# Expert inputs of a mixture-of-experts layer: rows fetched by an indirect DMA in place of one-hot products, and the overflow loop moved behind expert 1

## The chip, the cores and the metric

The program runs on one core of one Trainium2 chip. The metric is device time in microseconds (us) of one execution. The core has TensorE (PE in the profile, with its weight loads as PEld), VectorE (DVE), ScalarE (ACT), GpSimd (POOL) and SyncE (SP), 16 DMA engines that move data between HBM and the on-chip memory SBUF, and the accumulator memory PSUM, which PE writes.

## The reference

A network of four layers on 512 tokens of width 1024, all in float32: two layers of a first block, then two layers of a second block. Only the end of a second-block layer matters here:

```
x = layer_norm(a * x + mix, ln1_g, ln1_b)              # 512 x 1024
f = grouped_moe(x, w_router, router_bias, w_gate, w_up, w_down)
x = layer_norm(a * x + f, ln2_g, ln2_b)
```

`grouped_moe` computes softmax scores over 16 experts in 4 groups, takes the group with the best expert, in it the two best experts for each token, and weights them by their normalised scores. Each expert computes `(silu(x @ w_gate[e]) * (x @ w_up[e])) @ w_down[e]` on its tokens, with `w_gate` and `w_up` 1024 x 512 and `w_down` 512 x 1024. A token's two results, times their weights, are added. Any expert may have any number of tokens; none is dropped.

## The kernel before

Every float32 product is split in three: a value is written as a rounded part h (ACT, `hi`) plus a rest l (DVE, `lo`), and PE computes h*h + h*l + l*h (`mm3`). Weights are split as they arrive.

A second-block layer has two phases. `mix` ends with the product with w_out, the layer norm's statistics, the router and `after_mix` (line 1396), once for token tiles 0 and 1 and once for tiles 2 and 3 (`late`). `after_mix` normalises a tile on ACT, applies the layer norm's scale and shift along the free axis with broadcast tiles, mostly on POOL (`AFFINE`, line 41), and splits the result into `x1` (h and l, 128 tokens x 1024). `route` (line 1507) finds each token's experts and its rank within each expert: `rank` (128 x 4 x 16), ready at the instruction `self.ranked`; then the number of overflow blocks `ovi`, ready at `self.routed`. In layer 0 the second `mem_kv` (keys and values of the memory for layer 1) lies beside it on PE.

`moe` (line 1677) gives each expert a block of 128 rows ("slots") of a DRAM tensor `yd`. Tokens of rank over 128 go to overflow blocks behind the 16 experts' own. First 10 weight chunks of 512 KB are asked for (`first`). Then the overflow loop (line 1688, `For_i` over a count that is read from SBUF into registers of all engines) runs once per overflow block: it gathers tokens, loads the block's expert weights into buffers of its own, and writes its result to `yd`. At the end of the loop, also after no turn at all, all engines wait for each other and for all DMAs in flight.

The gather is `expert_in` (line 1629): for two experts at a time POOL builds a one-hot matrix from `rank` (`expert_slots`), and PE multiplies the tokens' h and l parts by it,

```
nc.tensor.matmul(pt[:, u * n:(u + 1) * n], xs[i][part][:, f], oh[:, i], ...)
```

that is 8 feature tiles x 4 token tiles x 2 parts = 64 products of 256 columns, which leave the two experts' tokens transposed in PSUM. They are split again into `xT`. It stands once ahead of expert 0 and then ahead of each even expert for the next two.

The experts are then walked in order: `expert_up(e)` (48 products of 512 columns in three passes each over 8 feature tiles for gate and up, 4 transposes of the hidden values) and `expert_down(e - 1)` (24 products, two stores of 256 KB into `yd` from ACT's queue). So an expert has 12 weight chunks of 512 KB, 6 products for each. They are loaded by SP's queue, in program order, into 9 buffers: 5 of the tag `mr` and 4 of `wr`; a load waits until its buffer was split by ACT (line 1616) and DVE (line 1617).

At expert 14 POOL adds the two parts of the tokens again into `f` (line 1724), the residual. Expert 15's rows are combined without `yd`; for the others 8 indirect DMAs of POOL (line 1751) fetch each token's two rows of `yd`, and DVE and PE add them, weighted, to `f`.

The framework keeps each engine's instructions near program order, moves up what is ready where an earlier one would wait, and adds the semaphores. `tc.issue_after(x)` keeps an instruction behind x on its engine. What stands behind the loop in the program is not moved ahead of it.

Of the kernel before, what the change touches and what calls it, by code (L numbers as in the profile page):

```python
# [18 lines left out]
P = 128  # L19
T = 512  # L20
D = 1024
# [11 lines left out]
N_OV = 7  # L33
# [4 lines left out]


G, V = ("gpsimd", "gpsimd"), ("vector", "vector")  # L40
AFFINE = ((G, G), (G, G)), ((G, G), (G, V))
T2 = (26, 29, 45, 26)


def slopes(n):
# [3 lines left out]
class K:  # L49
# [1346 lines left out]
    def after_mix(self, l, xs, i0, gb, pl, sc, x1):  # L1396

        nc = self.nc
        tt = nc.vector.tensor_tensor
        st = self.ln_stats(xs[i0:i0 + 2])  # L1400
        u = self.small([2, 16], name="ru2")
        bc = lambda v: v[:, :, None].to_broadcast([P, 2, 16])
        bt = lambda v: v[:, None, :].to_broadcast([P, 2, 16])
        tt(u, bt(self.wsum[:, l, 0]), bc(st[:, 2]), op=OP.mult)
        tt(u, u, bt(self.wsum[:, l, 1]), op=OP.add)
        yield
        c = slice(i0, i0 + 2)
        tt(sc[:, c], pl[:, i0 * 16:(i0 + 2) * 16].rearrange("p (i e) -> p i e", i=2), bc(st[:, 1]), op=OP.mult)
        tt(sc[:, c], sc[:, c], u, op=OP.add)
        yield  # L1410
        late = i0 > 0
        for a in range(2):
            x = xs[i0 + a]
            t = self.x2()
            self.normal(x, st, a)
            for v in range(2):
                eng = AFFINE[late][a][v]
                with self.tc.issue_after(self.ranked.ins) if late else nullcontext():
                    getattr(nc, eng[0]).tensor_tensor(t[v], x[v], gb[0][v], op=OP.mult)  # L1419
                    getattr(nc, eng[1]).tensor_tensor(t[v], t[v], gb[1][v], op=OP.add)  # L1420
            h, lo = [self.wp.tile([P, D], F32R, name="x1", tag="xt", bufs=8) for _ in range(2)]
            x1[i0 + a] = h, lo
            for v in range(2):
                o = slice(v * 512, (v + 1) * 512)
                self.hi(h[:, o], t[v])
                with self.tc.issue_after(self.routed.ins) if late else nullcontext():
                    self.lo(lo[:, o], t[v], h[:, o])

    def moe_constants(self):
        nc, cp = self.nc, self.cp  # L1430
# [12 lines left out]
                                channel_multiplier=-1)  # L1443
# [4 lines left out]
        ap = self.I["router_bias_2"]  # L1448
# [7 lines left out]
        for l in range(2):  # L1456
            for j, name in enumerate(("ln1_g_2", "ln1_b_2")):
                v = self.vec[name, 0][:, l * 8:(l + 1) * 8, None].to_broadcast([P, 8, 16])
# [6 lines left out]
                if j:  # L1465
                    nc.vector.tensor_tensor(s, s, rb, op=OP.add)
        self.yd = self.dp.tile([SLOTS, D], F32, name="yd")

    def clear_slots(self):

# [155 lines left out]
    def f4(self, dt=F32R, name="f4"):  # L1626
        return self.ph.tile([P, D], dt, name=name, tag="f4", bufs=6)

    def expert_in(self, xs, oh, n):

        nc = self.nc
        xT = []
# [12 lines left out]
    def expert_slots(self, rank, e, eng):  # L1645

        oh = self.f4(F32R, "oh").rearrange("p (i a s) -> p i a s", i=4, a=2)
        for a in range(2):
            for i in range(4):
                eng.tensor_scalar(oh[:, i, a], self.iota, rank[:, i, e + a:e + a + 1], None, op0=OP.is_equal)  # L1650
        return oh.rearrange("p i a s -> p i (a s)")

    def expert_up(self, xT, wg, wu):

# [22 lines left out]
    def moe(self, l, xs, rt):  # L1677
# [6 lines left out]

        cur = self.small([P], name="cur", bufs=1)
        nc.vector.tensor_scalar(cur, self.iota, 16.0 * P - 1.0, None, op0=OP.add)
        nov = nc.values_load(ovi[0:1, 7:8], min_val=0, max_val=N_OV)
        with tc.For_i(0, nov, 1) as b:
            ev = nc.values_load(ovi[0:1, bass.ds(b, 1)], engines=[mybir.EngineType.SP], min_val=0, max_val=15)
            row = b * P + 16 * P  # L1690
            we = [w[bass.ds(ev, 1)].rearrange("o k c -> (o k) c") for w in W]
            oh = self.f4(F32R, "oh").rearrange("p (i a s) -> p i a s", i=4, a=2)
            for i in range(4):
                nc.vector.tensor_scalar(oh[:, i, 1], cur, slotf[:, 0, i:i + 1], None, op0=OP.is_equal)
                nc.vector.scalar_tensor_tensor(oh[:, i, 0], cur, slotf[:, 1, i:i + 1], oh[:, i, 1].bitcast(F32),  # L1695
                                               op0=OP.is_equal, op1=OP.add)
            nc.vector.tensor_scalar(cur, cur, float(P), None, op0=OP.add)
            xT = self.expert_in(xs, oh.rearrange("p i a s -> p i (a s)"), 256)
            hT = self.expert_up([[v[:, :P] for v in t] for t in xT], self.wrows(we[0], 8, True), self.wrows(we[1], 8, True))
            self.expert_down(hT, we[2], self.yd[bass.ds(row, P)], True)  # L1700
        oh = self.expert_slots(rank, 0, nc.vector)
        xT = self.expert_in(xs, oh, 256)
        hT = None
        f = []
        for e in range(16):
            if e % 2 == 0 and e < 14:
                oh = self.expert_slots(rank, e + 2, nc.gpsimd)
                nx = self.expert_in(xs, oh, 256)
            if e == 15:
                self.expert_down(hT, W[2][14], self.yd[14 * P:15 * P])  # L1710
            o = e % 2 * P
            h2 = self.expert_up([[v[:, o:o + P] for v in t] for t in xT],
                                *[self.wrows(W[j][e], 8, first=first.pop(0) if first else None) for j in range(2)])
            if e == 2:
                slot, wv, wl = self.weigh(oh1, oh2, sc, slotf)
            if e == 13:
                after = self.last_pe
            if e == 14:
                for i in range(4):
                    with tc.issue_after(after.ins):  # L1720
                        f.append(self.x2())
                        for h in range(2):
                            o = slice(h * 512, (h + 1) * 512)
                            nc.gpsimd.tensor_tensor(f[i][h], xs[i][0][:, o].bitcast(F32), xs[i][1][:, o].bitcast(F32), op=OP.add)
# [3 lines left out]
            if e % 2:  # L1728
                xT = nx

        pt = self.pt()
        for i in range(4):
            nc.tensor.transpose(pt[:, i * P:(i + 1) * P], oh[:, i, P:].bitcast(F32), self.ident)
        ct = self.t2(F32R, "ct")
        nc.scalar.copy(ct, pt)
        pw = self.pt()
        for i in range(4):
            nc.tensor.matmul(pw[:, :1], oh[:, i, P:].bitcast(F32), wl[:, i:i + 1], start=i == 0, stop=i == 3)
        dg = self.t2(F32, "dg")
        for i in range(2):  # L1740
            for j in range(2):
# [14 lines left out]
        def add(i, j):  # L1756
            for h in range(2):
                if (i, h) in ON_PE:
                    continue
                nc.vector.scalar_tensor_tensor(f[i][h], gs[2 * i + j][:, half[h]], wv[:, j, i:i + 1], f[i][h],  # L1760
                                               op0=OP.mult, op1=OP.add)
# [9 lines left out]
                nc.vector.tensor_tensor(f[i][h], f[i][h], ps, op=OP.add)  # L1771

        y = []
        for c in range(2):
            py = self.pj()
            ws2 = list(self.wsplit(raws[c]))
            if c:
                for i in range(2):
                    for j in range(2):
                        add(i, j)  # L1780
# [186 lines left out]
```

## Time and profile before

| | |
|---|---|
| three runs | 3029.88, 3032.44, 3035.55 us; median 3032.44 |
| the profiled execution | 3038.98 us, span 3037.2 us, mean granted TensorE clock 0.981 |
| busy in the span | PE 95%, PEld 81%, DVE 64%, ACT 51%, POOL 9% |
| expert products | layer 0 from 1617 to 1955 us, layer 1 from 2619 to 2995 us |
| overflow blocks | none in layer 0, one in layer 1 |

PE's busy time counts overlapping instructions once and includes their pipeline, so a gapless PE reads as 100%. "DMA share" is the busy time of the 16 DMA engines as a share; it can exceed 1 by a little, since packets overlap. PEclk 1.00 is 2.4 GHz, and 0.50 is 1.2 GHz.

### The profile page before, as it was taken

To read this page: it belongs to the slowest core of one execution; us is meant where nothing else is said; L and a number is where in the kernel's file an instruction comes from. 1 tells how busy PE (TensorE), PEld (TensorE's weight loads), DVE (VectorE), ACT (ScalarE), POOL (GpSimd) and SP (SyncE) were. 2 spreads that over 40 slices of the span, in tenths; PEclk is the share of its full clock that TensorE was granted. 3 is DMA by queue.
4 is the path that set the end of the run, shared out by engine and by line. 5 is a ranking of instruction groups with operands and counts; after the bars stand their busy time and mean duration, and the time that the engine had idled before them with its cause. 6 is when DMAs were issued, how large, how long until landed. Compare 5 with 4: busy or idle time off the path is not lost. (4 is left out here: it accounts for less than half of the span.)

```text
span 3037.2 us, 44080 instructions
## 1 busy us (share of the span) xinstructions
PE 2896.9 (95%) x16635; PEld 2454.0 (81%) x16635; DVE 1951.3 (64%) x3817; ACT 1557.7 (51%) x2717; POOL 271.0 (9%) x282
## 2 busy tenths in 40 slices
PE   8999999999999999999989999879999999699996
PEld 6888878876669998878888888669987878588874
DVE  4454467576656776444477878978744345777788
ACT  4343377466655455223345777535542244476774
POOL 0000000000000000000027000440000000260023
PEclk9999999999999999999999999989999999899998
DMA  4242325431026222322365988931223335378996
GB/s 133 85 148 81 105 84 160 141 91 36 25 84 205 70 60 66 97 88 80 103 201 196 330 320 322 320 98 59 64 78 96 90 111 167 112 277 302 326 324 239
DMA packets 335599, 453.48 MB, mean 149 GB/s; under 512 B 24374, under 2 KB 208408, under 8 KB 335384
## 3 DMA queue, kind: packets, MB, share of 16 engines
q1 hardware_dynamic: 320856, 421.78, 42.1%
q10 hardware_dynamic: 12224, 20.46, 1.8%
q0 software_dynamic: 2304, 8.39, 0.8%
q8 instruction: 132, 2.16, 0.3%
q14 instruction: 83, 0.68, 0.1%
HBM read 421.69 MB, written 28.88 MB: 148 GB/s over the span
## 5 line engine op out<-in xcount | busy, mean ns | idle before, releaser
L164 DVE TENSOR_TENSOR wl<-wr,wh 128x1024 fp32r<-128x1024 f32 x348 | 422.9, 1217 | 441.1 <-ACT wh L163 436.9
L163 ACT CAST wh<-wr 128x1024 fp32r<-128x1024 f32 x352 | 363.1, 1033 | 579.9 <-PE pj L185 336.6
L184 PE MATMUL pj<-x,wh 128*128 128x512 f32 x1288 | 508.2, 395 | 0.6 <-ACT x L110 0.6
L185 PE MATMUL pj<-x,wh 128*128 128x512 f32 x1288 | 507.6, 394 | 0.0
L186 PE MATMUL pj<-x,wl 128*128 128x512 f32 x1288 | 506.3, 393 | 1.1 <-DVE wl L164 1.0
L186 PEld LDWEIGHTS pj<-x,wl 128*128 128x128 f32 x1288 | 241.9, 188 | 54.9 <-issue 4.7
L184 PEld LDWEIGHTS pj<-x,wh 128*128 128x128 f32 x1288 | 242.0, 188 | 52.6 <-issue 4.6
L185 PEld LDWEIGHTS pj<-x,wh 128*128 128x128 f32 x1288 | 242.0, 188 | 52.3 <-issue 5.6
L211 PE MATMUL pj<-wh,x 128*128 128x256 f32 x864 | 249.1, 288 | 3.8 <-DVE xb L277 3.1
L212 PE MATMUL pj<-wl,x 128*128 128x256 f32 x864 | 247.2, 286 | 0.0
L213 PE MATMUL pj<-wh,x 128*128 128x256 f32 x864 | 245.3, 284 | 0.0
L211 PE MATMUL pj<-wh,yh 128*128 128x256 f32 x640 | 181.6, 284 | 0.5 <-ACT wh L163 0.3
L212 PE MATMUL pj<-wl,yh 128*128 128x256 f32 x640 | 179.6, 281 | 1.5 <-DVE wl L164 1.5
L213 PE MATMUL pj<-wh,yl 128*128 128x256 f32 x640 | 179.1, 281 | 0.4 <-DVE yl L127 0.3
L211 PEld LDWEIGHTS pj<-wh,x 128*128 128x128 f32 x864 | 166.3, 193 | 5.2 <-DVE xb L277 3.5
L212 PEld LDWEIGHTS pj<-wl,x 128*128 128x128 f32 x864 | 166.6, 193 | 0.4
L213 PEld LDWEIGHTS pj<-wh,x 128*128 128x128 f32 x864 | 166.3, 193 | 0.3
L1639 PE MATMUL pt<-oh,x 128*128 128x256 f32 x1088 | 136.2, 287 | 18.4 <-DVE oh L1695 8.6
L1617 DVE TENSOR_TENSOR wl<-mr,wh 128x1024 fp32r<-128x1024 f32 x106 | 139.1, 1312 | 22.3 <-ACT wh L1616 22.2
L1639 PEld LDWEIGHTS pt<-oh,x 128*128 128x128 f32 x1088 | 135.3, 195 | 20.2 <-DVE oh L1695 8.7
L1617 DVE TENSOR_TENSOR ml<-mr,mh 128x1024 fp32r<-128x1024 f32 x108 | 135.9, 1258 | 21.5 <-ACT mh L1616 19.4
L1419 POOL TENSOR_TENSOR x<-x,bc 128x512 f32<-128x512 f32 x14 | 18.2, 1321 | 1255.7 <-ACT x L1328 1255.7
(503 smaller groups left out, 6607.0 us busy)
## 6 DMA issues: line engine op xcount, KB each, us to landing
wr<-in_w_in SPq DMA_DIRECT2D x124, 512.0 KB, 3.7
mr<-in_w_exp_gate SPq DMA_DIRECT2D x76, 512.0 KB, 6.6
mr<-in_w_exp_up SPq DMA_DIRECT2D x72, 512.0 KB, 5.5
mr<-in_w_exp_down SPq DMA_DIRECT2D x66, 512.0 KB, 5.9
wr<-in_w_exp_down SPq DMA_DIRECT2D x62, 512.0 KB, 6.3
wr<-in_hawk_w_in SPq DMA_DIRECT2D x60, 512.0 KB, 3.6
wr<-in_w_exp_up SPq DMA_DIRECT2D x56, 512.0 KB, 4.4
wr<-in_w_exp_gate SPq DMA_DIRECT2D x52, 512.0 KB, 6.9
```

What stands on the lines that cost most here:

```text
L163: self.nc.scalar.copy(wh[:, :kt, :c], raw[:, :kt, :c])
L164: eng.tensor_tensor(wl[:, :kt, :c], raw[:, :kt, :c], wh[:, :kt, :c].bitcast(F32), op=OP.subtract)
L184: mm(ps, a[0], b[0], start=first, stop=False)
L185: mm(ps, a[0], b[1], start=False, stop=False)
L186: mm(ps, a[1], b[0], start=False, stop=last)
L211: mm(d, tok(x[k][0]), w[k][0][:, :n], start=k == 0 and a == 0, stop=False, skip_group_check=True)
L212: mm(d, tok(x[k][0]), w[k][1][:, :n], start=False, stop=False, skip_group_check=True)
L213: mm(d, tok(x[k][1]), w[k][0][:, :n], start=False, stop=end, skip_group_check=True)
L1419: getattr(nc, eng[0]).tensor_tensor(t[v], x[v], gb[0][v], op=OP.mult)
L1617: self.nc.vector.tensor_tensor(wl, raw, wh.bitcast(F32), op=OP.subtract)
L1639: nc.tensor.matmul(pt[:, u * n:(u + 1) * n], xs[i][part][:, f], oh[:, i], start=i == 0 and part == 0, stop=i == 3 and part == 1)
```

## The change

Experts 2 to 15 get their tokens from DRAM. `after_mix` splits the normalised tokens, without scale and shift, for `x1`; after that it applies scale and shift in place (multiplication on DVE, addition on POOL) and stores the tokens in a DRAM tensor `x1d` by SP's queue. `slot_tokens` turns ranks into the token of each slot (DVE, 8 small products on PE), `expert_fetch` fetches an expert's 128 rows of 4 KB by an indirect DMA of POOL, and `expert_turn` transposes them on PE, 8 transposes for an expert. Fetches go two experts ahead. Experts 0 and 1, and the overflow blocks, still use `expert_in`, on normalised tokens; scale and shift are applied there on the way out of PSUM, where features lie on partitions. The overflow loop stands ahead of expert 2's products. `f` is loaded from `x1d` by SP. The phase's pool of 2 KB tiles has 21 in place of 26 buffers.

```diff
@@ after_mix
+        order = lambda: self.tc.issue_after(self.ranked.ins) if late else nullcontext()
         for a in range(2):
             x = xs[i0 + a]
-            t = self.x2()
             self.normal(x, st, a)
-            for v in range(2):
-                eng = AFFINE[late][a][v]
-                with self.tc.issue_after(self.ranked.ins) if late else nullcontext():
-                    getattr(nc, eng[0]).tensor_tensor(t[v], x[v], gb[0][v], op=OP.mult)
-                    getattr(nc, eng[1]).tensor_tensor(t[v], t[v], gb[1][v], op=OP.add)
...
-                self.hi(h[:, o], t[v])
-                with self.tc.issue_after(self.routed.ins) if late else nullcontext():
-                    self.lo(lo[:, o], t[v], h[:, o])
+                self.hi(h[:, o], x[v])
+                with order():
+                    self.lo(lo[:, o], x[v], h[:, o])
+        for a in range(2):
+            x = xs[i0 + a]
+            with order():
+                self.affine(x, x, gb, nc.vector, nc.gpsimd)
+            self.put(self.x1d[l], i0 + a, x)
@@ expert_in
-            h, lo = self.split(pt[:, :2 * n], 1.0, "xg")
+            t = self.ph.tile([P, 512], F32, name="xb", tag="xb", bufs=2)
+            for u in range(2):
+                c, src, j = t[:, u * n:(u + 1) * n], pt[:, u * n:(u + 1) * n], l * 8 + k + u
+                if u:
+                    nc.vector.tensor_scalar(c, src, g[:, j:j + 1], b[:, j:j + 1], op0=OP.mult, op1=OP.add)
+                else:
+                    nc.scalar.activation(c, src, AF.Identity, scale=g[:, j:j + 1], bias=b[:, j:j + 1])
+            h, lo = self.split(t[:, :2 * n], 1.0, "xg")
@@ new
+    def slot_tokens(self, ohs, rank):
...
+        for j, oh in enumerate(ohs):
+            tt(a, oh, rank, op=OP.mult)
+            nc.vector.tensor_reduce(r[:, j], a, axis=AX.X, op=OP.add)
+            for u in range(2):
+                tt(tk[:, j, :, u], oh, tok[:, u], op=OP.mult)
+            for i in range(4):
+                nc.vector.tensor_scalar(at[:, j, i], self.iota, r[:, j, i:i + 1], None, op0=OP.is_equal)
+        for j in range(2):
+            for i in range(4):
+                nc.tensor.matmul(ps[:, :32], at[:, j, i], tk[:, j, i].rearrange("p u e -> p (u e)"),
+                                 start=j == 0 and i == 0, stop=j == 1 and i == 3)
...
+    def expert_fetch(self, l, idx, e):
+        xg = self.ph.tile([P, D], F32, name="xg", tag="xg", bufs=2)
+        self.nc.gpsimd.indirect_dma_start(out=xg, out_offset=None, in_=self.x1d[l],
+                                          in_offset=bass.IndirectOffsetOnAxis(ap=idx[:, e:e + 1], axis=0))
+        return xg
+    def expert_turn(self, xg):
+        xT = []
+        for h4 in range(2):
+            pt = self.pt()
+            for k in range(4):
+                f = (4 * h4 + k) * P
+                self.nc.tensor.transpose(pt[:, k * P:(k + 1) * P], xg[:, f:f + P], self.ident)
+            h, lo = self.split(pt, 1.0, "xg")
...
@@ moe
-        nov = nc.values_load(ovi[0:1, 7:8], min_val=0, max_val=N_OV)
-        with tc.For_i(0, nov, 1) as b:
...
-        oh = self.expert_slots(rank, 0, nc.vector)
-        xT = self.expert_in(xs, oh, 256)
+        def overflow():
+            nov = nc.values_load(ovi[0:1, 7:8], min_val=0, max_val=N_OV)
+            with tc.For_i(0, nov, 1) as b:
...
+        oh = self.expert_slots(rank, 0, 2, nc.vector)
+        xT = [... for xT in [self.expert_in(l, xs, oh, 256)] for a in range(2)]
+        idx = self.slot_tokens((oh1, oh2), rank)
+        fetched = {e: self.expert_fetch(l, idx, e) for e in (2, 3)}
         for e in range(16):
-            if e % 2 == 0 and e < 14:
-                oh = self.expert_slots(rank, e + 2, nc.gpsimd)
-                nx = self.expert_in(xs, oh, 256)
+            if e == 2:
+                overflow()
+            if e == 12:
+                oh = self.expert_slots(rank, 15, 1, nc.gpsimd)
+            if 0 < e < 15:
+                xT.append(self.expert_turn(fetched.pop(e + 1)))
+                if e < 13:
+                    fetched[e + 3] = self.expert_fetch(l, idx, e + 3)
...
             if e == 14:
-                for i in range(4):
-                    with tc.issue_after(after.ins):
-                        f.append(self.x2())
-                        for h in range(2):
-...
+                f = [self.load_x(self.x1d[l], i) for i in range(4)]
```

## Rows read from the trace of the kernel before

**Rows 1.** Stretches, all instructions: us, busy (count) PE, PEld, DVE, ACT, POOL, PEclk, DMA share, GB/s.
```profile
1661.90:1686.50 24.60, 24.60 (x141) 21.32 (x141) 18.41 (x19) 16.63 (x21) 6.09 (x6) 1.00 0.88 301
1686.50:1703.60 17.10, 17.10 (x78) 13.82 (x77) 15.32 (x15) 14.29 (x17) 0.00 (x0) 1.00 1.02 374
1728.30:1745.40 17.10, 17.10 (x78) 13.82 (x77) 15.31 (x15) 14.24 (x17) 0.00 (x0) 1.00 1.03 376
1755.00:1760.00 5.00, 5.00 (x24) 4.03 (x23) 3.49 (x4) 3.44 (x4) 0.00 (x0) 1.00 0.22 79
1775.00:1780.00 5.00, 5.00 (x23) 4.06 (x22) 4.19 (x5) 4.02 (x6) 0.00 (x0) 1.00 1.05 406
1670.00:1900.00 230.00, 228.98 (x1173) 191.93 (x1173) 183.37 (x176) 170.65 (x198) 0.00 (x0) 1.00 0.91 324
2800.00:2840.00 40.00, 40.00 (x210) 33.80 (x209) 31.88 (x32) 29.49 (x36) 0.00 (x0) 1.00 0.95 342
```
**Rows 2.** A stretch, line 1639 alone: us, busy (count) PE, PEld, PEclk, DMA share, GB/s.
```profile
1703.60:1745.40 41.80, 7.70 (x64) 7.68 (x64) 1.00 0.91 329
```
**Rows 3.** PE's timeline, layer 0: start, us, instruction, count, idle before and what ended it.
```profile
1594.79 0.21 PE L1530 MATMUL ps<-rsel,tri 128*128 128x64 bf16 x1 [6.05 <-DVE rsel L1527]
...
1612.06 0.28 PE L213 MATMUL pj<-wh,mx 128*128 128x256 f32 x1
1617.62 0.80 PE L1639 MATMUL pt<-oh,x 128*128 128x256 f32 x2 [5.28 <-ACT mh L1616]
...
1658.97 0.60 PE L1664 MATMUL pt<-ident,hs 128*128 128x128 f32 x4
1659.33 0.48 PE L184 MATMUL pj<-mh,hh 128*128 128x512 f32 x1
...
1954.59 0.66 PE L1664 MATMUL pt<-ident,hs 128*128 128x128 f32 x4 [0.78 <-DVE hs L1661]
```
**Rows 4.** PE's timeline, layer 1.
```profile
2619.09 0.79 PE L1639 MATMUL pt<-oh,x 128*128 128x256 f32 x2 [8.59 <-DVE oh L1695]
...
2649.00 0.39 PE L186 MATMUL pj<-mh,hl 128*128 128x512 f32 x1
2653.89 1.43 PE L1639 MATMUL pt<-oh,x 128*128 128x256 f32 x5 [4.50 <-DVE oh L1650]
...
2994.80 0.66 PE L1664 MATMUL pt<-ident,hs 128*128 128x128 f32 x4 [0.78 <-DVE hs L1661]
```
**Rows 5.** ACT's timeline at the end of the overflow loop, layer 1.
```profile
2649.43 0.58 ACT L1674 COPY yo<-pj 128x512 f32<-128x512 f32 x1 [1.73 <-PE pj L186]
2650.04 0.36 ACTq L1675 DMA_DIRECT2D yd<-yo  x1
2652.59 1.28 ACT L1616 ACT_TABLE_LOAD   x1 [2.57 <-DMA yd<-yo]
```
**Rows 6.** Weight chunks of tag mr: ns min/median/max, first and last start; last line us.
```profile
L1616 ACT CAST mh<-mr x108: 1037/1051/1058, 1616.3 to 2994.1; 128x1024 fp32r<-128x1024 f32 x108
L1617 DVE TENSOR_TENSOR ml<-mr,mh x108: 1210/1225/2314, 1617.6 to 2995.8; 128x1024 fp32r<-128x1024 f32 x108
...
DMA to landing us min/median/max: 4.0/6.2/7.9
```
**Rows 7.** The indirect DMAs of line 1751, columns as in Rows 6.
```profile
L1751 POOL DMA_INDIRECT yg<-yd,rslot x16: 933/1014/2107, 1949.2 to 3004.4; - x16
...
DMA to landing us min/median/max: 5.2/5.8/8.3
```
**Rows 8.** DVE's timeline in the router of layer 1.
```profile
2600.89 1.31 DVE L1483 TENSOR_TENSOR rt<-rsc,rq 128x64 f32<-128x64 f32 x1
...
2608.72 0.23 DVE L1483 TENSOR_TENSOR rt<-rt,rq 128x64 f32<-128x64 f32 x1
```
**Rows 9.** POOL's timeline beside it, the first and the last of 4 entries (6 instructions).
```profile
2600.85 1.26 POOL L1419 TENSOR_TENSOR x<-x,bc 128x512 f32<-128x512 f32 x1 [10.99 <-ACT x L1328]
...
2605.87 2.48 POOL L1420 TENSOR_TENSOR x<-x,bc 128x512 f32<-128x512 f32 x2
```

More of the change, by code (lines that the diff above doesn't have):

```diff
@@ L1467, in moe_constants @@
         self.yd = self.dp.tile([SLOTS, D], F32, name="yd")
+        self.x1d = [self.dp.tile([T, D], F32, name=f"x1d{l}") for l in range(2)]
     def clear_slots(self):
@@ L1627, in f4, with expert_in @@
         return self.ph.tile([P, D], dt, name=name, tag="f4", bufs=6)
-    def expert_in(self, xs, oh, n):
+    def expert_in(self, l, xs, oh, n):
         nc = self.nc
+        g, b = [self.vec[v, 0] for v in ("ln1_g_2", "ln1_b_2")]
         xT = []
@@ L1640, in expert_in, with expert_slots @@
                                          stop=i == 3 and part == 1)
-            h, lo = self.split(pt[:, :2 * n], 1.0, "xg")
+            t = self.ph.tile([P, 512], F32, name="xb", tag="xb", bufs=2)
[6 more added lines that the diff above has]
+            h, lo = self.split(t[:, :2 * n], 1.0, "xg")
             xT += [(h[:, u * n:(u + 1) * n], lo[:, u * n:(u + 1) * n]) for u in range(2)]
         return xT
-    def expert_slots(self, rank, e, eng):
-        oh = self.f4(F32R, "oh").rearrange("p (i a s) -> p i a s", i=4, a=2)
-        for a in range(2):
+    def expert_slots(self, rank, e, n, eng):
+        oh = self.f4(F32R, "oh")[:, :4 * n * P].rearrange("p (i a s) -> p i a s", i=4, a=n)
+        for a in range(n):
             for i in range(4):
@@ L1701, in moe @@
-        oh = self.expert_slots(rank, 0, nc.vector)
-        xT = self.expert_in(xs, oh, 256)
+        def overflow():
+            nov = nc.values_load(ovi[0:1, 7:8], min_val=0, max_val=N_OV)
+            with tc.For_i(0, nov, 1) as b:
+                ev = nc.values_load(ovi[0:1, bass.ds(b, 1)], engines=[mybir.EngineType.SP], min_val=0, max_val=15)
+                row = b * P + 16 * P
+                we = [w[bass.ds(ev, 1)].rearrange("o k c -> (o k) c") for w in W]
+                oh = self.f4(F32R, "oh").rearrange("p (i a s) -> p i a s", i=4, a=2)
+                for i in range(4):
+                    nc.vector.tensor_scalar(oh[:, i, 1], cur, slotf[:, 0, i:i + 1], None, op0=OP.is_equal)
+                    nc.vector.scalar_tensor_tensor(oh[:, i, 0], cur, slotf[:, 1, i:i + 1], oh[:, i, 1].bitcast(F32),
+                                                   op0=OP.is_equal, op1=OP.add)
+                nc.vector.tensor_scalar(cur, cur, float(P), None, op0=OP.add)
+                xT = self.expert_in(l, xs, oh.rearrange("p i a s -> p i (a s)"), 256)
+                hT = self.expert_up([[v[:, :P] for v in t] for t in xT], self.wrows(we[0], 8, True), self.wrows(we[1], 8, True))
+                self.expert_down(hT, we[2], self.yd[bass.ds(row, P)], True)
@@ L1703, in moe @@
+        oh = self.expert_slots(rank, 0, 2, nc.vector)
+        xT = [[[v[:, a * P:(a + 1) * P] for v in t] for t in xT] for xT in [self.expert_in(l, xs, oh, 256)] for a in range(2)]
+        idx = self.slot_tokens((oh1, oh2), rank)
+        fetched = {e: self.expert_fetch(l, idx, e) for e in (2, 3)}
         hT = None
-        f = []
         for e in range(16):
-            if e % 2 == 0 and e < 14:
-                oh = self.expert_slots(rank, e + 2, nc.gpsimd)
-                nx = self.expert_in(xs, oh, 256)
+            if e == 2:
[6 more added lines that the diff above has]
+                    fetched[e + 3] = self.expert_fetch(l, idx, e + 3)
@@ L1709, in moe @@
             if e == 15:
                 self.expert_down(hT, W[2][14], self.yd[14 * P:15 * P])
-            o = e % 2 * P
-            h2 = self.expert_up([[v[:, o:o + P] for v in t] for t in xT],
-                                *[self.wrows(W[j][e], 8, first=first.pop(0) if first else None) for j in range(2)])
+            h2 = self.expert_up(xT[e], *[self.wrows(W[j][e], 8, first=first.pop(0) if first else None) for j in range(2)])
             if e == 2:
                 slot, wv, wl = self.weigh(oh1, oh2, sc, slotf)
-            if e == 13:
-                after = self.last_pe
@@ L1737, in moe @@
         for i in range(4):
-            nc.tensor.matmul(pw[:, :1], oh[:, i, P:].bitcast(F32), wl[:, i:i + 1], start=i == 0, stop=i == 3)
+            nc.tensor.matmul(pw[:, :1], oh[:, i].bitcast(F32), wl[:, i:i + 1], start=i == 0, stop=i == 3)
         dg = self.t2(F32, "dg")
@@ L1777, in moe @@
             if c:
-                for i in range(2):
-                    for j in range(2):
-                        add(i, j)
+                with tc.issue_after(mark.ins):
+                    for i in range(2):
+                        for j in range(2):
+                            add(i, j)
             for k, wk in enumerate(ws2):
```

40 lines of the change are left out of this document (21 added, 19 removed).

## The prediction

> **What bounds the kernel now.** I read the page's parts 1 and 2 first: PE is busy 95% of the span, and only in the expert stages are the DMA engines above 0.8. Then the stretches between one expert's first store into `yd` and the next one's [rows 1]. They alternate. With a gather in it an expert takes 24.6 us and PE runs 141 instructions; without, 17.1 us and 78: 72 products, 4 transposes and 2 at the edges. PE is busy to the last digit in both, so PE sets the pace: (17.1 - 0.36) / 72 = 0.2325 us for a product of 512 columns at clock 1.00, where 0.36 us are four transposes (1658.97 to 1659.33) [rows 3]. The 64 gather products take 7.7 us [rows 2], some 7.5 net. A pair of experts takes 41.7 us.
>
> The reader should see how close the DMA engines are behind. In the 17.1 us halves they move 374 and 376 GB/s at a share of 1.02 to 1.03 and don't quite keep up: an expert consumes 12 x 0.524 = 6.29 MB and stores 0.52 MB, that is 398 GB/s. They recover in the other half; there the buffers get full and the share falls to 0.22 with PE still 100% busy [rows 1]. The gather is the DMA engines' rest.
>
> **The change part by part.**
>
> *Gathers out, transposes in.* Of the 8 pair gathers of a layer 7 go: 7 x 7.5 = 52.5 us of PE. 14 experts get 8 transposes, 8 x 0.09 to 0.11 = 0.8 us each, 11 us. PE alone would gain 41 us a layer, 82 in both, at 17.9 us an expert. The splits stay equal (two of 512 columns an expert, before four a pair). DVE with its 15.3 us plus two splits, and ACT with 14.3 plus two, stay under 17.9 [rows 1].
>
> *DMA.* Each fetch adds 0.52 MB: 7.34 MB an expert. At PE's 17.9 us that would need 410 GB/s, more than the best 5 us show (406) [rows 1]. So **the pace goes over from PE to the DMA engines**. The rate is the term that decides. I take 375, which two whole 17.1 us stretches show with the queue never empty: 19.6 us an expert, against 20.9 now. Ends: 406 from the best 5 us, 324 from the mean of 230 us, which includes the full-buffer dips.
>
> *The loop behind expert 1.* Engines enter it without a barrier, but leave it together, after all DMAs. In layer 1 PE's last product there is at 2649.0 and its next at 2653.9 [rows 4]: copy 0.6, store issued at 2650.04, landing about 2.1 later, release 0.5 after that [rows 5]: 3.1 us from the end of the products to the release. Before, nine buffers of weights waited behind that barrier. Now SP may not ask for expert 2's weights until the release: issue 0.4, landing at least 4.0, cast 1.05, rest 1.2 [rows 6]. PE idles about 3.1 + 6 us in each layer, and the DMA-paced part starts with no lead. The fetch of expert 4 in flight and expert 3's transposes are hidden in that idle time. In layer 0, where the loop has no turn, its barrier disappears from the start (5.28 us idle [rows 3]).
>
> *Ahead of expert 0.* The router's chain no longer runs beside POOL's scale and shift: 1.31 us beside POOL, 0.23 for the same line after it [rows 8, 9]. Six such operations make some 5.5 us. But the late scale and shift now follow `rank`, beside the h/l rests and the one-hots that the gather waits for: up to 5 us back. Bounds 0 and 5.5; I take 3. In layer 0 it shortens the 6.05 us wait [rows 3]. One pair gather stands ahead of expert 0 in place of two. Its scale and shift out of PSUM and `slot_tokens`' 8 products with some 16 DVE operations of 0.2 us, in part in waits, cost 2 us before expert 0. The fetch for expert 2 (POOL 1 us, landing 5.8, at most 8.3 [rows 7]) has expert 0's 11.5 us; the stores of `x1d` start some 8 us before that.
>
> *`f` from DRAM.* 2.1 MB more on SP, in the DMA sum; POOL's additions go, and with them a PE wait that the DMA-paced stretch would hide anyway. 8 tiles of 2 KB must be free among 21; the last of them perhaps only when expert 14's inputs are done, with SP's weights behind them. Bounds 0 and 9 us (half of an expert's time); I take 3 a layer.
>
> **The sum,** against the profiled execution (3038.98 us, span 3037.2, 6.5 above the median).
>
> From the release to the end of expert 15's up products SP and the others move 14 x 8 + 14 x 4 = 168 chunks (88.1 MB), 14 stores of 0.52 (7.3), 11 fetches (5.8) and `f` (2.1): 103.3 MB, at 375 GB/s 275.5 us. With issue 0.4, latency 2.1, cast and rest 2.3, the last six products 1.4 and the hidden product 0.7: 282.4, with `f`'s 3 us 285.4.
>
> - Layer 0: PE ends `mem_kv` at 1612.35 [rows 3], less 3: 1609.4. Gather and its tail 9.5: 1618.9. Two ups (2 x 11.52), one down (5.58), 8 transposes: 29.5: 1648.4. Release 3.1: 1651.5. Plus 285.4: 1936.9, against 1954.6 [rows 3]: -17.7.
> - Layer 1: start 2618.3 - 3 = 2615.3; 3 us for a clock that is at 0.5 after the router; 9.5; 29.5: 2657.3. The overflow turn 31.1 as before (2618.3, when its one-hots start, to 2649.4): 2688.4. Release: 2691.5. Plus 285.4: 2976.9, against 2994.8 [rows 4]: -17.9.
>
> What follows (fetching the rows of `yd`, the last expert, the norm) is kept. 35.6 us less: 3003.4 beside this execution, **2997 us** beside the median.
>
> By the Trainium skill (DMA: Bandwidth & Descriptors, section Bandwidth) the HBM side binds a core at about 358 GB/s. The 374 and 376 [rows 1] are above that for a whole half period, so the row decides; by the page the DMA part would be 288.5 us and the time 3023. It is the second rival, as a rate of this kernel.
>
> **Rivals.** Each layer's gain is 17.8 - (103.3 / rate - 275.5), so the time at another rate follows.
>
> 1. *PE keeps the pace.* It needs over 400 GB/s throughout. For: fetches move 4 KB rows, and 406 was reached. Against: no longer stretch has it. PE would take 14 x 17.1 + 13 x 0.9 = 251 and 5 us of restart: 47 us a layer, 2938.
> 2. *The writes and fetches cost the rate,* about 358 instead of 375. For: 342 in the best of the 40 us stretches [rows 1]. Against: those contain dips from full buffers. 288.5 in place of 275.5: 9.6 us less: 3023.
> 3. *Slower: the DMA engines have lost their rest and run at 342 or less behind a cold restart.* Place: from the loop's release to expert 15. Price: 302.0 at 342 GB/s, 318.8 at 324: 17 or 51 us over before, 3050 or 3083. It decides from 103.3 / 293.3 = 352 GB/s downwards. For: no 40 us of the trace are above 342, and the sum starts with nothing loaded. Against: PE was 100% busy in the dips, so demand, not the engines, made them.
> 4. *The fetch is not the gain it says,* since indirect rows land late and PE waits for them. Against: two experts, 39 us, lie between a fetch and its use, and 8.3 us is the longest landing [rows 7]. It would first show at expert 2, at a price of a few us.
>
> **How the numbers follow.** Forecast (362 to 390 GB/s: gains of 6.9 to 28.4 a layer, 3019 to 2976): 0.50. Rival 1: 0.08. Rival 2 (350 to 362): 0.20, of which 0.07 within 0.2% of before and the rest faster. Rival 3: 0.17. Rival 4, mixed with a longer hold at `f`: 0.05, a few us off the forecast, 0.01 of it not faster. 0.2%, some 6 us, is what a measurement can tell from no change. Faster: 0.50 + 0.08 + 0.13 + 0.04 = 0.75; same 0.07; slower 0.17 + 0.01 = 0.18. The likeliest case's own range is 2976 to 3019; the range over cases, 2958 to 3042, leaves out most of rival 1 and the larger half of rival 3, and takes in the bounds of the start (5.5 - 3 a layer) and of `f` (0 to 9).
>
> **What would show it.** Right: between experts 3 and 13 stores come every 19 to 20.5 us without alternation, DMA share 1.0 or more at 365 to 385 GB/s, casts waiting for DMA, PE under 95% busy; 9 us of idle PE ahead of expert 2 in both layers; 192 gather products in place of 1088; expert 15's end 18 us earlier, counted from each layer's router. Wrong: PE full at 18 us an expert (rival 1); a DMA share of 1.0 at 355 or less (rivals 2 and 3); a share under 0.9 with PE waiting, which would mean a queue held back (SP at `f`, or too few buffers), not the engines; transposes that wait for a fetch (rival 4). Half clock on PE between experts would also break it, as short waits then cost twice.

## The result, and the profile after

The changed kernel takes 2988.97 us (median of 4 runs, 2987.34 to 2993.22) where the kernel before took 3031.85 beside it: ratio 0.9859, 95% interval 0.9842 to 0.9876, 42.9 us less. Measured again with the second group of experiments it took 2990.12, ratio 0.9851 (0.9838 to 0.9865). Its profiled execution is 2993.22 us long, span 2991.5, mean granted clock 0.974: 45.7 us less than the profiled execution of before. The forecast was 2997, and 3003.4 beside the profiled execution.

The page's second part of the changed kernel, 40 slices of 74.8 us each:

```profile
PE   7999999999999999999997999879999999789995
PEclk9999999999999999999998999989999999899997
DMA  4242324431016322223265999932122334479995
GB/s 135 86 146 86 101 90 144 141 106 43 26 33 224 94 62 67 85 92 93 91 206 190 345 391 393 337 120 71 58 78 92 99 106 144 146 274 394 391 391 202
```

Slices 23 to 26 and 36 to 39 are the expert stages. Whole slices stand at 391 to 394 GB/s. Two stretches between the stores of neighbouring experts, one of 230 us and one of layer 1, in the columns of [rows 1]:

```profile
1701.90:1720.20 18.30, 18.30 (x88) 14.74 (x86) 16.52 (x17) 15.44 (x20) 0.94 (x1) 1.00 1.05 392
1720.20:1738.30 18.10, 18.10 (x87) 14.70 (x85) 15.65 (x16) 14.07 (x18) 0.94 (x1) 1.00 1.05 393
1670.00:1900.00 230.00, 230.00 (x1057) 184.61 (x1056) 207.25 (x201) 188.63 (x225) 10.37 (x10) 1.00 1.05 392
2800.00:2840.00 40.00, 40.00 (x186) 31.99 (x185) 36.31 (x36) 32.32 (x40) 1.87 (x2) 1.00 1.05 393
```

The alternation is gone: in layer 0 the second stores of neighbouring experts lie 18.0 to 18.4 us apart from expert 2's to expert 13's, PE is busy to the last digit, and the DMA share is 1.05 throughout, where [rows 1] had 0.91 in the same 230 us. The gather products fell from 1088 to 192, and 224 transposes came (groups of the kernel after: count, busy us, mean ns, idle before):

```profile
L1709 PE MATMUL pt<-ident,xg 128*128 128x128 f32 x224 | 30.9, 284 | 9.1 <-issue 5.6 <-DMA xg<-x1d,idx 3.5
...
L1642 PE MATMUL pt<-oh,x 128*128 128x256 f32 x192 | 27.2, 307 | 16.8 <-DVE oh L1660 14.0 <-DVE xb L1648 2.8
```

PE's timeline of layer 0, after, the counterpart of [rows 3]; expert_in is now L1642, expert_turn L1709, the transposes of the hidden values L1725:

```profile
1586.77 0.19 PE L1531 MATMUL ps<-rsel,tri 128*128 128x64 bf16 x1 [0.43 <-DVE rsel L1528]
...
1597.84 0.55 PE L210 MATMUL pj<-wh,mx 128*128 128x256 f32 x1 [8.52 <-DVE mkl L124]
...
1614.20 7.80 PE L1642 MATMUL pt<-oh,x 128*128 128x256 f32 x64 [0.67 <-DVE oh L1660]
...
1639.86 1.97 PE L1709 MATMUL pt<-ident,xg 128*128 128x128 f32 x8 [3.52 <-DMA xg<-x1d,idx]
...
1660.73 1.09 PE L1709 MATMUL pt<-ident,xg 128*128 128x128 f32 x8 [1.88 <-issue]
...
1663.07 0.80 PE L184 MATMUL pj<-wl,xgh 128*128 128x512 f32 x1 [0.76 <-DVE wl L1618]
...
1907.55 0.50 PE L183 MATMUL pj<-mh,hh 128*128 128x512 f32 x1 [0.78 <-ACT mh L1617]
...
1931.47 1.11 PE L1725 MATMUL pt<-ident,hs 128*128 128x128 f32 x4 [8.26 <-DVE hs L1722]
```

And of layer 1, beside [rows 4]:

```profile
2573.80 1.96 PE L1505 MATMUL ps<-wrg,xr 128*128 128x16 f32 x16 [0.24 <-ACT xr L1500]
2582.13 0.21 PE L1531 MATMUL ps<-rsel,tri 128*128 128x64 bf16 x1 [6.37 <-DVE rsel L1528]
2595.89 10.12 PE L1642 MATMUL pt<-oh,x 128*128 128x256 f32 x64 [13.30 <-DVE oh L1660]
...
2645.05 3.48 PE L1642 MATMUL pt<-oh,x 128*128 128x256 f32 x16 [2.81 <-DVE xb L1648]
...
2673.62 1.97 PE L1709 MATMUL pt<-ident,xg 128*128 128x128 f32 x8 [3.69 <-issue]
...
2944.52 1.11 PE L1725 MATMUL pt<-ident,hs 128*128 128x128 f32 x4 [7.74 <-DVE hs L1722]
```

The milestones of the prediction. Layer 1 is given with 23.3 us added, the shift that layer 0 leaves behind (the router's logits begin at 2573.80, before at 2597.09). The prediction counted layer 1's start from the one-hots (2618.3), 0.8 us ahead of the gather's first product (2619.09 [rows 4]); the column after has the product:

| | before | predicted | after |
|---|---|---|---|
| layer 0: gather starts | 1617.6 | 1609.4 | 1614.2 |
| loop's release | | 1651.5 | 1660.7 |
| expert 15's transposes | 1954.6 | 1936.9 | 1931.5 |
| layer 1: start | 2618.3 | 2615.3 | 2619.2 |
| loop's release | | 2691.5 | 2696.9 |
| expert 15's transposes | 2994.8 | 2976.9 | 2967.8 |
| end of the execution | 3038.98 | 3003.4 | 2993.2 |

Where the 45.7 us come from, by the transposes of experts 2, 14 and 15: from expert 2 to expert 14 layer 0 takes 219.2 us in place of 249.3 and layer 1 220.0 in place of 252.6, together 62.7 less. From expert 14 to 15 it takes 33.5 and 34.1 in place of 21.9 each, 23.8 more. The ways up to expert 2 are 4.6 and 6.6 us shorter, the tail after the last transposes 4.6 longer, the rest 0.2.

A wait that the prediction did not know stands at the end of the stage in each layer: 8.26 and 7.74 us of idle PE ahead of expert 15's transposes. VectorE's timeline there, after, layer 0:

```profile
1920.49 1.23 DVE L1618 TENSOR_TENSOR ml<-wr,mh 128x1024 fp32r<-128x1024 f32 x1 [0.18 <-ACT mh L1617]
1928.93 0.75 DVE L1819 SCALAR_TENSOR_TENSOR x<-yg,rw,x 128x512 f32<-128x512 f32 x1 [7.22 <-DMA yg<-yd,rslot]
1929.60 1.22 DVE L1618 TENSOR_TENSOR wl<-mr,wh 128x1024 fp32r<-128x1024 f32 x1
1930.74 0.68 DVE L1722 TENSOR_TENSOR hs<-hs,pj 128x512 f32<-128x512 f32 x1
```

An addition of a fetched row of `yd` (L1819), which stands behind `hs` in the program, was put ahead of it. VectorE waits 7.22 us for that row, with a split of weights and `hs` behind it. In the kernel before the wait ahead of the same transposes was 0.78 us [rows 3, 4].

### The profile page after: what moved, and what is told of

It is laid out like the page before. It is cut to its first block, busy times and chain, and to the rows that moved or that the text cites. A ratio compares the mean times of both kernels' runs of the same rounds, so it can differ in the third digit from the quotient of the medians.

```text
span 2991.5 us, 42712 instructions
## 1 busy us (share of the span) xinstructions
PE 2835.3 (95%) x15979; PEld 2377.3 (79%) x15979; DVE 1944.8 (65%) x3877; ACT 1548.3 (52%) x2725; POOL 151.6 (5%) x182
## 5 line engine op out<-in xcount | busy, mean ns | idle before, releaser
L1618 DVE TENSOR_TENSOR wl<-mr,wh 128x1024 fp32r<-128x1024 f32 x106 | 129.3, 1220 | 26.6 <-ACT wh L1617 26.0
L1617 ACT CAST mh<-mr 128x1024 fp32r<-128x1024 f32 x108 | 112.9, 1048 | 27.3 <-PE pj L185 13.8
L211 PEld LDWEIGHTS pj<-wl,yh 128*128 128x128 f32 x640 | 121.9, 191 | 1.9 <-DVE wl L163 1.5
L210 PEld LDWEIGHTS pj<-wh,yh 128*128 128x128 f32 x640 | 121.7, 190 | 1.1 <-ACT yh L113 0.4
```

The source lines that it names most:

```text
L210: mm(d, tok(x[k][0]), w[k][0][:, :n], start=k == 0 and a == 0, stop=False, skip_group_check=True)
L211: mm(d, tok(x[k][0]), w[k][1][:, :n], start=False, stop=False, skip_group_check=True)
L1617: self.nc.scalar.copy(wh, raw)
L1618: self.nc.vector.tensor_tensor(wl, raw, wh.bitcast(F32), op=OP.subtract)
```

## Experiments

Ratios are to the kernel before on the same chip, with 95% intervals; the changed kernel stands at 0.9851 to 0.9859. "Period" is the time from expert 2's to expert 14's transposes, divided by 12; the changed kernel's is 18.26 in layer 0 and 18.33 in layer 1.

**VectorE's order at expert 15** (`mark` is the split of expert 15's hidden values).

```diff
-        for i in range(2, 4):
-            add(i, 0)
+        with tc.issue_after(mark.ins):
+            for i in range(2, 4):
+                add(i, 0)
```

> The changed kernel with one constraint more: the additions of fetched rows for token tiles 2 and 3 stay behind expert 15's split on VectorE. Theory A, VectorE's order: in the changed kernel one such addition stands on VectorE ahead of expert 15's product of silu and up and waits there for a row of yd, and PE idles 8.26 us (layer 0) and 7.74 us (layer 1) ahead of the last transposes. With it behind, the transposes follow the products by 0.8 us as in the kernel before, 7 to 8 us earlier in each layer; the last two rows are asked for only when a buffer is split, which comes earlier too: 10 to 16 us less than the changed kernel, 2973 to 2979. Theory B, the rows set the end: the last row is asked for at 1936.9 and lands some 5 us later, so PE only waits further back: 0 to 3 us less.

2979.79 us, ratio 0.9812 (0.9798 to 0.9825). PE's timeline of this kernel:

```profile
1918.77 0.66 PE L1725 MATMUL pt<-ident,hs 128*128 128x128 f32 x4 [0.78 <-DVE hs L1722]
...
1972.05 0.58 PE L210 MATMUL pj<-wh,x 128*128 128x256 f32 x1 [3.10 <-DVE xb L276]
```

The wait is 0.78 us again, and expert 15 comes 26.2 and 26.9 us after expert 14 in place of 33.5 and 34.1. Theory A holds. By the ratios the edit is worth 12 us beside the repeated changed kernel, with intervals that don't overlap. Not all of the earlier transposes stays: from layer 0's to the rank's product of layer 1 655.6 us pass in place of 650.0 in the repeated run, 2.8 of the 5.6 at layer 1's first product (3.10 us idle, there 0.29). And some 6 of the 14 us between these two profiles arise ahead of expert 2 in layer 0, where the edit changes nothing: there PE waits 1.88 us for the first fetch in place of 3.15, and the granted clock of the next 10 us is 0.83 in place of 0.71. So some 9 us of the profiles are the edit's.

**Which of PE and the DMA engines sets the pace.** Less for the DMA engines:

```diff
+        rows = dict(fetched)
+        rows = [rows[2], rows[3]]
...
-                    fetched[e + 3] = self.expert_fetch(l, idx, e + 3)
+                    fetched[e + 3] = rows[(e + 3) % 2]
```

> The changed kernel without the fetches for experts 4 to 15 (they are given the rows of experts 2 and 3, so 12 indirect transfers of 0.52 MB a layer are left out). Theory A, PE keeps the pace and the nine buffers cover the little that the DMA engines lack: stores still come every 18.2 to 18.3 us between experts 3 and 13; only the 2 us of small waits in expert 15's products go: 0 to 5 us less than 2989. Theory B, the DMA engines set the pace at 391 GB/s: 6.82 MB need 17.4 us, so the period falls to what PE alone needs, 17.9 or less, and 8 us or more are gained; at the 375 GB/s of the prediction 7.34 MB would need 19.6, and all the difference to 18.2 would show.

Less for PE (`two` is set for the down products of experts 2 to 14):

```diff
 mm3
-        mm(ps, a[0], b[1], start=False, stop=False)
-        mm(ps, a[1], b[0], start=False, stop=last)
+        mm(ps, a[0], b[1], start=False, stop=last and self.two)
+        if not self.two:
+            mm(ps, a[1], b[0], start=False, stop=last)
...
```

> The changed kernel without the third pass of the down products of experts 2 to 14 (the rest of the hidden values is not multiplied): 64 products of 0.2325 us in place of 72, PE needs 1.9 us less an expert, 16.4. Theory A, the DMA engines are right behind PE: 7.34 MB at 391 GB/s need 18.8 us, the stock in the buffers is soon used up and PE waits for casts: stores every 18.0 to 18.8 us after the first few experts, the time within 8 us of 2989. Theory B, the share of 1.05 only shows that transfers are always queued, and the engines have room: 16.6 to 17.2 us (VectorE's 16.6 is next), 28 to 45 us less.

More for the DMA engines, first into a spare buffer:

```diff
 expert_fetch
+        x2 = self.f4(F32, "x2")
+        self.nc.gpsimd.indirect_dma_start(out=x2, out_offset=None, in_=self.x1d[l],
+                                          in_offset=bass.IndirectOffsetOnAxis(ap=idx[:, e:e + 1], axis=0))
```

> The changed kernel with every fetch done twice (the second copy goes to a spare buffer and is not read): 7.86 MB an expert. Theory A, the DMA engines at 391 GB/s are at their limit: 20.1 us an expert once the stock of some five chunks (2.6 MB) is used up, 1.8 us more for 11 experts in two layers less 2 x 6 us of stock: 25 to 40 us more than 2989, PE waits for casts from about the sixth expert on. Theory B, they have room: the period stays at 18.3 and the time within 5 us of 2989.

then, in a later run, with `out=xg` in place of `out=x2`:

> The changed kernel with every fetch done twice into the same buffer, one after the other, so that the second copies are spread over the experts (in e4_fetch_twice all of them went out ahead of expert 3, and the experts after it ran at 18.4 us as before): 7.86 MB an expert in place of 7.34. Theory A, the DMA engines are at their limit near 392 GB/s as the kernel with less work for PE showed: 19.5 to 20.1 us an expert once the stock in the buffers is used up, PE waits for casts; 20 to 40 us slower than the changed kernel's 2990. Theory B, they have room and PE alone sets 18.3 us: within 6 us of it.

| | period, layer 0 / 1 | us | ratio |
|---|---|---|---|
| fetches left out | 18.26 / 18.29 | 2979.74 | 0.9813 (0.9798 to 0.9828) |
| PE 1.9 us less | 18.54 / 18.45 | 3000.22 | 0.9874 (0.9859 to 0.9890) |
| fetched twice, spare buffer | 19.37 / 19.34 | 3023.39 | 0.9959 (0.9943 to 0.9975) |
| fetched twice, same buffer | 19.40 / 19.44 | 3034.07 | 0.9995 (0.9985 to 1.0004) |

The same 200 us (columns of [rows 1]) of the kernel without fetches,

```profile
1700.00:1900.00 200.00, 198.49 (x907) 158.43 (x905) 176.24 (x171) 160.48 (x193) 0.00 (x0) 1.00 1.02 369
```

of the one with less work for PE, and what its PE waited for (total us, times, longest),

```profile
1700.00:1900.00 200.00, 185.12 (x820) 140.36 (x819) 177.53 (x173) 161.84 (x194) 8.16 (x9) 1.00 1.04 390
```

```profile
PE pj L185 <- DVE ml L1620: 7.9, 11, 0.8
PE pj L184 <- ACT mh L1619: 5.4, 10, 0.6
```

and of the one that fetches twice into the same buffer:

```profile
1700.00:1900.00 200.00, 191.30 (x867) 149.21 (x865) 169.08 (x163) 154.81 (x185) 23.51 (x18) 1.00 1.05 395
```

With less to move the period stays: PE sets it in the changed kernel. With less for PE it stays too: PE is idle for 15 of 200 us and waits for splits of chunks that land late (ScalarE, which makes the first part of a split, waits 26 us for chunks there). Why it even rises a little is not shown. With 7.86 MB the steady experts (8 to 12 in layer 0) take 19.8 to 19.9 us, which is 396 GB/s, and PE is idle for 9 of 200 us. So the DMA engines' limit is near 396 GB/s, 18.5 us for 7.34 MB, and PE's 18.3: two limits 0.2 us apart.

That PE can run at 18.3 when 18.5 is needed I put down to the nine chunks (4.7 MB) loaded ahead. By an estimate from these rows, 7.34 MB in 18.37 us are 400 GB/s where 392 flow, so 230 us use up 1.8 MB of the stock. The changed kernel's trace agrees in the main: in layer 0 ScalarE waits for no chunk from 1661 to 1800, then 15 times from 1803 to 1877, 0.2 to 0.7 us each; in layer 1 seven times from 2688 to 2725 and steadily from 2796. The kernel without fetches has no such wait from 1700 to 1900.

The first form of fetching twice missed its aim: all its second copies went out by 1681.9, while expert 3 waited and took 31.1 us, and then an expert took 18.4 again. The kernel without fetches came out 9 us under 2989, 12 by the ratios to the repeated changed kernel, where theory A allowed 5. Of the 14.6 us between these two profiles 6 lie between the router and expert 2 in layer 0, where only one fetch is left out but PE waits 1.86 us for the first one in place of 3.15 and goes on at a clock of 1.00 in place of 0.71 (10 us), and 2.4 in both layers between experts 2 and 14.

**The loop's place.**

```diff
+        overflow()
         oh = self.expert_slots(rank, 0, 2, nc.vector)
...
-            if e == 2:
-                overflow()
```

> The changed kernel with the overflow loop back ahead of expert 0's gather, where it stood before; everything else of the change is kept. Theory A, the loop behind expert 1 costs little because SP's weight loads for expert 2 pass in front of it (nine chunks of them are issued before the branch in the trace): PE idles 1.9 + 0.8 us there in each layer; back at the start come the 5.3 us of idle PE in layer 0 and 4.5 us in layer 1 that the kernel before had: 4 to 9 us slower than the changed kernel. Theory B, the prediction's step, by which the loop behind expert 1 costs 9 us of idle PE a layer and the lead in weights: 8 to 13 us faster.

2993.99 us, ratio 0.9871 (0.9856 to 0.9886): slower than the repeated changed kernel's 0.9851 by 4 to 6 us, with intervals that overlap. PE's timeline has the two barriers back:

```profile
1614.81 5.36 PE L1642 MATMUL pt<-oh,x 128*128 128x256 f32 x29 [5.14 <-ACT mh L1617]
```

and 4.47 us in layer 1. Theory B, the prediction's 9 us a layer behind expert 1, is refuted. SP's timeline of the changed kernel shows why:

```profile
1636.48 0.37 SPq L1603 DMA_DIRECT2D mr<-in_w_exp_gate  x1
1637.61 6.28 SPq L1603 DMA_DIRECT2D wr<-in_w_exp_gate  x2
1647.04 0.37 SPq L1603 DMA_DIRECT2D mr<-in_w_exp_gate  x1
1648.18 0.37 SPq L1603 DMA_DIRECT2D wr<-in_w_exp_up  x1
1650.07 2.73 SPq L1603 DMA_DIRECT2D mr<-in_w_exp_up  x3
1655.19 0.37 SPq L1603 DMA_DIRECT2D wr<-in_w_exp_down  x1
1663.04 0.37 SPq L1603 DMA_DIRECT2D mr<-in_w_exp_down  x1
```

The nine chunks up to 1655.19 are expert 2's gate and up and the first of expert 1's down; the release is at 1660.7. The loads pass the loop, against what the description of the kernel before says.

**Expert 2's transposes.**

```diff
             if e == 2:
+                xT.append(self.expert_turn(fetched.pop(2)))
+                fetched[4] = self.expert_fetch(l, idx, 4)
                 overflow()
...
-            if 0 < e < 15:
+            if 1 < e < 15:
```

> The changed kernel with expert 2's transposes (and the fetch for expert 4 behind them) moved behind expert 1's up products and expert 0's down products. Theory A, the first fetch lands late: in layer 0 PE waits 3.52 us for it ahead of expert 1's products; moved, the wait goes: 2 to 4 us faster, all of it in layer 0. Theory B, the wait only moves on, since expert 1's weights land no earlier: within 1 us.

2995.65 us, ratio 0.9877 (0.9862 to 0.9892). Both theories missed. PE's timeline:

```profile
1649.46 1.03 PE L1709 MATMUL pt<-ident,xg 128*128 128x128 f32 x8
1656.96 1.97 PE L1709 MATMUL pt<-ident,xg 128*128 128x128 f32 x8 [6.46 <-issue]
...
1981.93 0.58 PE L210 MATMUL pj<-wh,x 128*128 128x256 f32 x1 [6.34 <-DVE xb L276]
```

The wait for the first fetch is gone (1649.46), but the fetch for expert 4 now starts at 1650.8 and lands at 1655.5, the loop's end waits for it, and 1.88 us (2.32 in the repeated run) became 6.46. Expert 2 is still 2.5 us sooner, counted from the router. More is lost at layer 1's first product, 6.34 us idle against 0.29 in the repeated changed kernel: its place behind VectorE's `xb` is another one, though nothing was edited there.

**The router's second half** (overflow blocks and slots, which the first gather doesn't need, into a function of its own that `moe` calls behind the first fetches; ranks are kept, `pos` is `rank - 1`):

```diff
 route
-        pos = ...; nov, inc, bse = ...; slotf = ...; ovi = ...
+        return oh1, oh2, sc, rank, count
 moe
         fetched = {e: self.expert_fetch(l, idx, e) for e in (2, 3)}
+        slotf, ovi = self.slots(oh1, oh2, rank, count)
```

> Three edits of the changed kernel: expert 15's split ahead of the late additions on VectorE (as in e1_order), expert 2's transposes behind expert 1 (as in e6_turn_late), and the second half of the router (overflow blocks and slots of yd, some 25 small VectorE operations) moved behind the first gather, which needs the ranks alone. Theory A, VectorE's queue ahead of the gather sets the start: in layer 1 the one-hots stand 12.2 us behind the rank (2582.5 to 2594.8), of which rests and scale and shift are some 5.5: 5 to 8 us earlier in layer 1, up to 5 in layer 0 where PE's mem_kv waits 8.5 us for VectorE. With 10 to 16 of e1_order and 2 to 4 of e6_turn_late: 2960 to 2975. Theory B, POOL's additions and the stores of tokens 2 and 3 set the start: the router's half is no loss, 2973 to 2979.

> The changed kernel once more, beside the three above on the same chip: 2985 to 2995, to compare them with; its start (PE's wait for the first fetch in layer 0) shows how far that wait varies from run to run: 0 to 4 us.

> e1_order with the second half of the router moved behind the first gather, and expert 2's transposes left where the change has them. In e7_best the gather started 2.9 us earlier in both layers, counted from the router's first product, and that was lost again. Theory A, what lost it was the later place of the transposes: 4 to 8 us less than e1_order (0.9812 of the kernel before; so 0.979 to 0.980). Theory B, the overflow turn then waits for the slots and layer 0's start for its fetch: within 3 us of e1_order.

With both other edits 2980.84 us (0.9830, 0.9817 to 0.9844), short of its forecast; PE idles 7.89 us at the loop's end of layer 0, where the kernel with only the transposes moved had 6.46. With VectorE's order alone 2978.32 (0.9809, 0.9795 to 0.9822), the lowest of all, but 1.5 us from VectorE's order without it (0.9812): theory B's bound holds. The unchanged repeat was as expected, 2990.12. The gather does start sooner; layer 1 of the last kernel:

```profile
2577.67 0.21 PE L1531 MATMUL ps<-rsel,tri 128*128 128x64 bf16 x1 [6.37 <-DVE rsel L1528]
2588.57 9.79 PE L1653 MATMUL pt<-oh,x 128*128 128x256 f32 x64 [10.44 <-DVE oh L1671]
```

10.9 us after the rank's product in place of 13.8, and the wait of `mem_kv` in layer 0 falls from 8.52 to 5.55. Counted from the rank's product, expert 2 comes 4.3 us sooner in layer 1 than with VectorE's order alone, but 0.8 later in layer 0, where PE idles 5.07 us at the loop's end in place of 2.34. That VectorE's queue held the gather is shown; that it is worth 4 us or more in the total is not.

**The loads of f,** behind the last weights, all of them and then half:

```diff
-                f = [self.load_x(self.x1d[l], i) for i in range(4)]
...
         raws = [self.wload(W[2][15][:, c * 512:(c + 1) * 512], 4) for c in range(2)]
+        f = [self.load_x(self.x1d[l], i) for i in range(4)]
```

> e1_order with the loads of f moved behind the last expert's weights on SP's queue. Theory A, the 2.1 MB of f in front of the last weights cost PE the 2 us of small waits in expert 15's products of each layer: 2 to 5 us less than e1_order (ratio 0.981 to the kernel before, so 0.980). Theory B, f is then late for the additions, since it competes with the rows of yd: VectorE waits for f, and the end of each layer comes 3 to 6 us later.

> e11_order_router with only the second half of f (token tiles 2 and 3, which are added last) loaded behind the last expert's weights, 1.05 MB instead of 2.1. In e10_f_behind_weights the waits in expert 15's products went (its transposes came 22.7 us behind expert 14's in place of 26.5), but the additions waited for rows of yd that landed later. Theory A, half of f in front keeps the early rows in time: 1 to 2 us of each layer gained, 2974 to 2977 (0.980 of the kernel before). Theory B, any f behind the weights delays the rows of yd by as much as it frees ahead: within 1.5 us of e11_order_router, 2978.

2980.26 us (0.9817, 0.9802 to 0.9833) and 2980.95 (0.9828, 0.9814 to 0.9841): no gain over their bases. With all of f behind, expert 15 follows expert 14 by 22.7 us in place of 26.2, so f costs 3.5 us there; but VectorE then waits (layer 1):

```profile
2938.36 3.40 DVE L1818 SCALAR_TENSOR_TENSOR x<-yg,rw,x 128x512 f32<-128x512 f32 x5 [5.95 <-DMA yg<-yd,rslot]
```

and the end after the last transposes takes 52.5 us in place of 45.9. The 2.1 MB are paid for on either side.

## Why the prediction was right in its number and wrong in four steps

*Gathers out, transposes in.* Right: 18.3 us an expert where PE alone was put at 17.9, and no gather left in the stage. The 8 transposes hold PE for 0.79 us, as taken. The 0.4 us are four products an expert that start 0.32 to 0.37 us behind the one before in place of 0.23; the kernel without fetches has them too.

*DMA, the term that decides.* Its size was wrong, and with it the pace-setter. I took 375 GB/s as the engines' limit because the queue seemed never empty. But the rows of 17.1 us are means. Inside the first of them the kernel before has a slow part and one at the rate that the engines hold now:

```profile
1687.00:1691.50 4.50, 4.50 (x22) 3.61 (x21) 3.70 (x4) 3.91 (x5) 0.00 (x0) 1.00 0.97 334
1691.50:1697.50 6.00, 6.00 (x28) 4.85 (x27) 5.19 (x6) 4.76 (x7) 0.00 (x0) 1.00 1.05 404
```

The rows of the prediction had a sign of it: the share was 1.02 to 1.03 at 374 and 376, and 1.05 at 406 [rows 1]. Now the share is 1.05 for 230 us at 392. From the release to the last up products of layer 0 (1660.7 to 1923.2) it took 262.5 us, predicted 285.4. Of the 22.9 us, 12.6 are the nine chunks that were loaded before the release (4.7 MB at 375), and 10.3 the rate: the 98.6 MB left, 262.9 us at 375, take 252.6 at 390. Rival 1, which had 0.08, was nearest in mechanism: PE kept the pace, at 18.3 and not 18.0, with the DMA engines just behind, and neither I nor that rival had seen that the buffers bridge the difference. The measured 392 lies above the 362 to 390 of the forecast and far above the rates of rivals 2 and 3, which fall. By the Trainium skill (DMA: Bandwidth & Descriptors, section Bandwidth) the HBM side binds such transfers at about 358 GB/s, which the same section gives as a core's share when both cores of a pair stream. The trace shows 392 over 230 us with one core running, so the measurement decides.

*The loop behind expert 1.* Wrong: SP's loads pass it. PE idles 1.88 and 0.76 us in layer 0 where 9 were taken. The overflow turn took 37.2 us (2636.4 to 2673.6) where 31.1 and 3.1 were taken, of it 2.81 for the scale and shift that VectorE does behind a split (2645.05).

*Ahead of expert 0.* Both bounds came true at once and cancelled. In layer 1 the rank's product stands 8.3 us behind the start of the logits, before 12.9 (the operation of 1.31 us in [rows 8] takes 0.22 now); then 13.8 us pass to the gather where it was 9.1. In layer 0 `mem_kv` waits 8.52 us for VectorE. I took a gain of 3; it was nothing in layer 1, and in layer 0 the gather started 4.8 us later than predicted.

*The first fetch,* held to be hidden by expert 0: wrong. PE waited 3.52 us for it in layer 0 (1.9 to 3.5 in the profiles that leave its place alone and fetch once, 0.2 with the loop first), and the granted clock of 1640 to 1650 was 0.73. The landings, 6.8 to 9.1 us in the trace, are somewhat over the 5.2 to 8.3 read before; the larger miss is when the fetch leaves. VectorE's and POOL's timelines:

```profile
1626.27 1.66 DVE L1684 TENSOR_SCALAR at<-iota,str 128x128 bf16<-128x128 f32 x8
...
1630.19 0.18 DVE L1692 TENSOR_TENSOR idx<-pt,idh 128x16 int32<-128x16 f32 x1
1631.33 1.20 POOL L1698 DMA_INDIRECT xg<-x1d,idx  x1 [30.29 <-PE pj L185]
```

Expert 0's first product is at 1621.8, and `slot_tokens` still stands among splits on VectorE, so the fetch goes out 9.5 us into expert 0. This is rival 4's sign, at its price of a few us, in one place.

*f from DRAM:* 3 us taken, 3.5 shown at expert 15.

*What follows is kept:* wrong. The order on VectorE at expert 15 costs 8 us of idle PE a layer, and PE comes back from that idle time mostly at half clock.

*The arithmetic:* by the formula above the rivals, 362 GB/s gives a gain of 7.9 us a layer and 3017 us, not 6.9 and 3019.

So the number 2997 stands 8 us from 2989 (10 in the profiled executions) because errors of both signs met: 23 and 22 us too much in the stages of the two layers, against 9 and 5 too little ahead of the release, 8 and 8 at expert 15, and 5 in the tail. That it came so near is luck. Of the prediction's signs of being right, the 192 gather products and the missing alternation came; PE full at 18 us an expert was the sign of rival 1, and transposes that wait for a fetch that of rival 4.

## What to carry to other kernels

The mean DMA rate of a stretch is not the engines' limit because the stretch looks busy. Look inside it, and compare its share with the highest of the trace: here 375 GB/s at 1.02 to 1.03 left room up to 392 to 396 at 1.05, and these few per cent decided who sets the pace. When an edit makes loads earlier than results, look at each engine's queue for an operation that now stands ahead of the critical one and waits: one line of order was worth some 9 us in the profiles and 12 by the ratios, about a quarter of the change itself. Two resources within a few per cent of each other are found by lightening each alone, where neither shortens the period, and by loading one more, which lengthens it.

## What the runs showed of the hardware that was not expected

The DMA engines held 392 GB/s over 230 us, and 395 with 4 KB rows fetched twice, with PE at full clock beside them.

An idle stretch of PE costs more than its length. After the 8.26 us the granted clock of the next 8.5 us is 0.57, mostly the 1.2 GHz level; in the kernel with VectorE's order, after 0.78 us, that of the next 9.2 us is 1.00, 2.4 GHz. The same stretch, first of the changed kernel, then of the other:

```profile
1931.50:1940.00 8.50, 8.50 (x30) 7.41 (x31) 6.20 (x8) 2.02 (x3) 6.24 (x6) 0.57 0.36 104
```

```profile
1918.80:1928.00 9.20, 8.21 (x40) 5.97 (x40) 7.17 (x10) 3.23 (x5) 8.30 (x8) 1.00 0.96 376
```

The end of a loop that makes no turn also waits for an indirect DMA issued just ahead of it: 6.46 and 7.89 us of idle PE, in the two kernels with expert 2's transposes moved, in place of 1.88.
